# Low parts of weights, of the first columns and the additions of norms: all on VectorE

## The chip, the core and the metric

The kernel runs as one program on one core of a Trainium2 chip. The metric is the device time of one execution in microseconds (us), the median over several runs. On the core five engines work side by side, each with its own queue of instructions: TensorE (PE in the profile; PEld is its weight load), VectorE (DVE), ScalarE (ACT), GpSimd (POOL) and SyncE (SP), which here only issues DMAs. An engine takes its queue in order and waits on semaphores for what other engines produce.

## The reference

A decoder trunk of two layers over 512 tokens of width 1024, in float32. Each layer is: a norm modulated by a condition `c`, a token mixer, a gated residual; then a modulated norm, a mixture of experts (16 experts, two for each token, SwiGLU of width 256), a gated residual. Layer 0 mixes by dilated attention in three head groups (48 heads of 64, one projection of 1024 to 9216 columns), layer 1 by forgetting attention (16 heads, projection to 3088 columns).

```python
for i in range(DEPTH):
    mod = (ada_in @ w_ada[i] + b_ada[i]).reshape(b, 6, d)
    ...
    hm = rmsnorm(x, norm_mix[i]) * (1 + sc_m) + sh_m
    y = dilated_mixer(hm, ...) if i % 2 == 0 else forgetting_mixer(hm, ...)
    x = x + g_m * y
    hf = rmsnorm(x, norm_ffn[i]) * (1 + sc_f) + sh_f
    x = x + g_f * hierarchical_moe(hf, ...)
```

## The kernel before, in words

Every large matrix product is made of three: an operand is split into a high part `hi`, the value rounded to a shorter format by an ACT copy, and a low part `lo` = value - `hi`, and PE adds hi by hi, lo by hi and hi by lo in one PSUM bank (`part`, lines 291 to 298; the line says which of the three a matmul is: 295, 296, 298). So each weight piece of 128 x 1024 that comes from memory needs one ACT instruction (line 150) and one subtraction (line 153) before PE can use it.

`Stream` (line 78) brings the weight pieces in a fixed order: `fetch` issues the DMA on SP's queue into one of a few buffers (`raw`, four of them, in the mixers; more kinds in the experts' stages), `split` makes `hi` and `lo` in six buffers each. A piece is split as soon as fewer than six split pieces are live, that is when PE has let go of an older one (`done`, which calls `fill`). The buffer `raw` is free for the next DMA when both the copy and the subtraction have read it. In the experts' stages all subtractions are on VectorE; in the mixers every second piece (odd `ns`) goes to GpSimd.

The four `raw` buffers also serve `ada` (line 384), a background job that computes the modulation rows: eight DMAs of `w_ada`, eight VectorE multiply-adds (line 394) into `acc`, then a hi/lo split of `acc` (lines 399 and 400) and four matmuls with a column of ones (lines 406 and 409). Ten such jobs run beside mixer A, one instruction group at every second step of the main work.

`begin` (line 301) is the start: x is transposed to columns `xT`, while VectorE adds up 32 half pieces of `w_ada` (line 361) for the first two modulation rows. When a half of them is in, `col` is made (lines 373 and 375), and for four of the eight column blocks ACT makes `hi` (line 378), VectorE the modulated value (line 379), and VectorE or GpSimd `lo` (line 380; GpSimd for blocks 0, 1, 3, 4, 6 and 7).

`normed` (line 420) is a norm over rows: square and sum on ACT, an inverse root in five small instructions (`rsqrt`, lines 215 to 219, two on ACT and three on VectorE, where line 217 multiplies a small tile by itself), a multiply on VectorE (428 or 431) and the addition of the shift row (432). `moe_norm` uses it for four row blocks ahead of each experts' stage, with the addition on GpSimd; the result goes to memory, from where each expert's rows are gathered. `mix_in` uses it for four row blocks of layer 1, with the addition on GpSimd for blocks 1 and 3; PE transposes the result (line 450). In the attention parts `qknorm` (line 458) uses the same `rsqrt` on 128 x 8 tiles.

GpSimd also issues the gathers and scatters of the experts (lines 1198 and 1240), clears `acc` (389), multiplies in the merge of mixer A (789) and does small routing work (1029 to 1182).

The order within each engine's queue is not simply that of the program text. The framework that builds the program simulates it with modelled times and puts, engine by engine, what is ready and first in program order next; where work of several row blocks is independent it ends up interleaved. `issue_after` binds an instruction behind another. So an instruction that moves to another engine may also shift its neighbours in the queues.

Of the kernel before, what the change touches and what calls it, by code (L numbers as in the profile page):

```python
# [8 lines left out]
F32 = mybir.dt.float32  # L9
# [4 lines left out]
OP = mybir.AluOpType  # L14
# [63 lines left out]
class Stream:  # L78
# [51 lines left out]
    def split(self):  # L130
        nc, t = self.t.nc, self.t
        _, n, kind = self.pieces[self.ns]
        tag, raw = self.raws.pop(self.ns)
        if kind == "down":

            self.whole[self.ns] = tag
            self.parts[self.ns] = (raw, None)
            self.ns += 1
            return
        self.held[tag] -= 1  # L140
        self.live += 1
        hi = t.w.tile([P, 1024], F32R, name="hi", tag="hi", bufs=6)
        lo = t.w.tile([P, 1024], F32R, name="lo", tag="lo", bufs=6)
        h, l, r = hi[:, :n], lo[:, :n], raw[:, :n]
        if kind[:3] == "out":

            g = t.g_m[:, int(kind[3:]):int(kind[3:]) + 512].unsqueeze(1).to_broadcast([P, n // 512, 512])
            rv = r.rearrange("p (k c) -> p k c", c=512)
            nc.vector.tensor_tensor(rv, rv, g, op=OP.mult)
        t.act = nc.scalar.activation(h, r, AF.Copy)  # L150
        on_v = kind == "moe" or self.ns % 2 == 0
        eng = nc.vector if on_v else nc.gpsimd
        eng.tensor_tensor(l, r, h.bitcast(F32), op=OP.subtract)  # L153
        self.parts[self.ns] = (hi, lo)
        self.ns += 1

# [21 lines left out]
class Trunk:  # L178
# [122 lines left out]
    def begin(self, sb, first):  # L301

        nc, i, V = self.nc, self.i, self.nc.vector
# [5 lines left out]
        xs = []  # L309
        for b in range(NB):  # L310
            x = self.k.tile([P, D], F32, name="big", tag="big", bufs=5)
# [20 lines left out]
        xT = sb.tile([P, KT, S], F32, name="xT")  # L332

        def rows():
            ss = self.small(NB, "ss4")
            for b in range(NB):
                sq = sb.tile([P, D], F32, name="sq0", tag="sq0", bufs=1)
                nc.scalar.activation(sq, xs[b], AF.Square, accum_out=ss[:, b:b + 1])
            V.tensor_scalar(ss, ss, 1.0 / D, EPS, op0=OP.mult, op1=OP.add)
            r = self.rsqrt(ss, NB)  # L340
            for b in range(NB):
                nc.scalar.activation(xs[b], xs[b], AF.Copy, scale=r[:, b:b + 1])
            for k in range(KT):
                t = self.bank("t")
                for b in range(NB):
                    nc.tensor.transpose(t[:, b * P:(b + 1) * P], xs[b][:, k * P:(k + 1) * P], self.ident)
                nc.scalar.activation(xT[:, k, :], t, AF.Copy)

        wv = i["w_ada"][0].rearrange("(k p) c -> p k c", p=P)
        for half in range(2):  # L350
            cs = slice(half * 512, half * 512 + 512)
            for n in range(2):
                for kk in range(0, KT, 2):
                    if (8 * half + 4 * n + kk // 2) % 11 < 6:
                        raw = self.k.tile([P, D], F32, name="mix", tag="mix", bufs=6)
                    else:
                        raw = sb.tile([P, D], F32, name="ada", tag="ada0", bufs=5)
                    raw = raw.rearrange("p (k c) -> p k c", c=512)
                    nc.sync.dma_start(out=raw, in_=wv[:, kk:kk + 2, (1 - n) * D + half * 512:(1 - n) * D + half * 512 + 512])
                    for k in range(2):  # L360
                        last = V.scalar_tensor_tensor(accs[n][:, cs], raw[:, k], self.csil[:, kk + k:kk + k + 1], accs[n][:, cs], op0=OP.mult, op1=OP.add)
                if half == 0 and n == 0:
                    rows()
            if half:
                self.early = self.project_early(first)
            c = slice(4 * half, 4 * half + 4)
            for n in range(2):
                t = self.bank("s")
                for k in range(4 * half, 4 * half + 4):
                    nc.tensor.matmul(t[:, k:k + 1], lhsT=accs[n][:, k * P:(k + 1) * P], rhs=self.ones[:, 0:1], start=True, stop=True)  # L370
                with self.tc.issue_after(last.ins):
                    if n == 0:
                        V.scalar_tensor_tensor(col[:, 0, c], t[:, c], 1.0, col[:, 0, c], op0=OP.add, op1=OP.mult)
                    else:
                        V.tensor_copy(col[:, 1, c], t[:, c])
            for k in range(4 * half, 4 * half + 4):
                hi, lo = self.h(k, slice(None))
                nc.scalar.activation(hi, xT[:, k, :], AF.Identity, scale=col[:, 0, k:k + 1], bias=col[:, 1, k:k + 1])
                V.tensor_scalar(xT[:, k, :], xT[:, k, :], col[:, 0, k:k + 1], col[:, 1, k:k + 1], op0=OP.mult, op1=OP.add)
                (V if k % 3 == 2 else nc.gpsimd).tensor_tensor(lo, xT[:, k, :], hi.bitcast(F32), op=OP.subtract)  # L380
            if half == 0:
                self.st.fill(2)

# [663 lines left out]
    def moe_norm(self, layer, sb, xs, b, after):  # L1047

        nc, m = self.nc, self.m
        nc.sync.dma_start(out=self.x_d[layer][b * P:(b + 1) * P, :], in_=xs[b])  # L1050
        hf = sb.tile([P, D], F32, name="hf", tag=("xh", "xl")[b], bufs=2) if b < 2 else m["xr"][b - 2]
        m["r", b] = self.normed(xs[b], m["a_f"], m["sh_f"], hf, hf, eng=nc.gpsimd, after=after)
        nc.sync.dma_start(out=self.hf_d[b * P:(b + 1) * P, :], in_=hf)

    def moe_turn(self, sb, xs, b, h):
# [273 lines left out]

    def mix_in(self, layer, b, sb, x, a, sh):  # L1330
        h = sb.tile([P, D], F32, name="hm", tag=("xh", "xl")[b % 2], bufs=2)
        self.normed(x, a, sh, h, h, eng=(self.nc.vector, self.nc.gpsimd)[b % 2])
        c = slice(b * P, (b + 1) * P)
        self.turned(h, 2, lambda k, tv: self.hilo(*(t[:, :, c] for t in self.hT[k // 2]), tv))

# [69 lines left out]
```

## Time and profile before

| what | us |
|---|---|
| median of 3 runs | 1470.24 (1465.14 to 1475.07) |
| the profiled execution | 1476.0 |
| its span on the core | 1474.2 |
| PE busy | 1328.8 (90%) |
| VectorE busy | 966.6 (66%) |
| ScalarE busy | 652.1 (44%) |
| GpSimd busy | 294.9 (20%) |

The span is the time from the first to the last instruction in the profile. Busy time is the union of the instructions' spans on an engine. Matmuls overlap each other, so a busy PE is not a PE at its peak, but where it is idle nothing is being multiplied. The stages in the span: the start to about 65 us, mixer A to 700, its experts to 940, the change to layer 1 to 985, mixer B to 1258, its experts to the end.

### The profile page before, as it was taken

The numbers are of one execution on the slowest core, as the hardware profiler recorded it, in microseconds if no ns is written. First come the engines' busy times: TensorE is split into PE (matmuls) and PEld (weight loads), VectorE is DVE, ScalarE is ACT, GpSimd is POOL, SyncE is SP. The second block draws the span as 40 slices with busy tenths as digits, with TensorE's granted clock in tenths as the row PEclk, the third lists the DMA queues.
The fourth block names the chain that finished last, engine by engine and source line by source line (L and its number), as shares of the span: only waits on it lengthen the run. The fifth ranks groups of instructions, "written<-read, shape, count | busy, mean of one in ns | idle before, by whom it ended". The sixth has DMA issues, their size and how long they took to land. (4 is left out here: it accounts for less than half of the span.)

```text
span 1474.2 us, 20070 instructions
## 1 busy us (share of the span) xinstructions
PE 1328.8 (90%) x7017; PEld 1075.1 (73%) x7017; DVE 966.6 (66%) x1841; ACT 652.1 (44%) x1356; POOL 294.9 (20%) x192
## 2 busy tenths in 40 slices
PE   5799999989998999999969998499999999799995
PEld 3688888868986988887756665268888878566663
DVE  6775766675666675664677775376766753877772
ACT  6333544344433453344245554344544542355551
POOL 2312111221121211110232221211111100332221
PEclk9899999999999999999979999799999999889998
DMA  9356444644454645254679998604222463799981
GB/s 358 117 174 203 143 138 139 192 124 153 145 156 158 188 131 176 68 187 132 232 257 302 283 294 253 179 17 123 72 66 86 133 197 125 253 293 311 306 279 24
DMA packets 187156, 264.15 MB, mean 179 GB/s; under 512 B 23064, under 2 KB 148696, under 8 KB 187046
## 3 DMA queue, kind: packets, MB, share of 16 engines
q1 hardware_dynamic: 160742, 227.86, 47.5%
q0 software_dynamic: 8576, 16.85, 4.9%
q10 hardware_dynamic: 17728, 18.05, 4.1%
q8 instruction: 59, 0.97, 0.3%
q14 instruction: 51, 0.42, 0.1%
HBM read 249.85 MB, written 25.43 MB: 187 GB/s over the span
## 5 line engine op out<-in xcount | busy, mean ns | idle before, releaser
L295 PE MATMUL ps_pj<-hi,h 128*128 128x512 f32 (+1 forms) x1016 | 395.5, 398 | 6.2 <-ACT h L455 3.3
L296 PE MATMUL ps_pj<-lo,h 128*128 128x512 f32 (+1 forms) x1016 | 375.6, 378 | 0.8 <-POOL lo L153 0.8
L298 PE MATMUL ps_pj<-hi,h 128*128 128x512 f32 (+1 forms) x1016 | 290.0, 375 | 5.5 <-POOL h L380 5.4
L153 POOL TENSOR_TENSOR lo<-raw,hi 128x1024 fp32r<-128x1024 f32 x56 | 139.9, 2498 | 620.3 <-ACT hi L150 567.2
L295 PEld LDWEIGHTS ps_pj<-hi,h 128*128 128x128 f32 x1016 | 239.7, 236 | 31.5 <-issue 6.6
L296 PEld LDWEIGHTS ps_pj<-lo,h 128*128 128x128 f32 x1016 | 241.1, 237 | 16.6 <-POOL lo L153 1.4
L298 PEld LDWEIGHTS ps_pj<-hi,h 128*128 128x128 f32 x1016 | 212.1, 236 | 27.3 <-POOL h L380 7.8
L394 DVE SCALAR_TENSOR_TENSOR acc<-ada,csil,acc 128x1024 f32<-128x1024 f32 x80 | 111.9, 1399 | 112.5 <-DMA ada<-in_w_ada 112.2
L150 ACT ACTIVATE hi<-raw 128x1024 fp32r<-128x1024 f32 x126 | 132.2, 1051 | 100.0 <-PE ps_pj L298 52.1
L153 DVE TENSOR_TENSOR lo<-raw,hi 128x1024 fp32r<-128x1024 f32 x70 | 102.8, 1471 | 33.0 <-ACT hi L150 30.0
L295 PE MATMUL ps_pj<-hi,xh 128*112 128x512 f32 x256 | 105.4, 412 | 0.0
L296 PE MATMUL ps_pj<-lo,xh 128*112 128x512 f32 x256 | 104.0, 406 | 0.0
L298 PE MATMUL ps_pj<-hi,xl 128*112 128x512 f32 x256 | 80.9, 397 | 0.0
L1237 DVE SCALAR_TENSOR_TENSOR y<-ps_s,r_ws,g_f 112x512 f32<-112x512 f32 x64 | 47.9, 748 | 35.0 <-PE ps_s L1236 35.0
L455 ACT ACTIVATE xh<-ps_t 128x448 fp32r<-128x448 f32 x64 | 31.8, 542 | 84.3 <-PE ps_t L450 84.3
L462 ACT ACTIVATE sq<-ps_pj 128x512 f32<-128x512 f32 x63 | 37.0, 589 | 61.8 <-PE ps_pj L298 50.9
L927 DVE CUSTOM_DVE_ANT_0 nl<-ps_s,cums 128x128 f32<-128x128 f32 (+1 forms) x64 | 31.0, 484 | 46.5 <-PE ps_s L925 43.4
L153 DVE TENSOR_TENSOR lo<-h,hi 128x1024 fp32r<-128x1024 f32 x42 | 51.1, 1223 | 15.6 <-ACT hi L150 14.7
L722 PEld LDWEIGHTS ps_o<-vr,pt 128*128 128x128 f32 x480 | 58.0, 192 | 1.4
L929 ACT ACTIVATE nl<-nl,mn 128x128 f32<-128x128 f32 (+1 forms) x64 | 35.8, 559 | 50.6 <-DVE mn L927 50.0
L722 PE MATMUL ps_o<-vr,pt 128*128 128x64 f32 x480 | 57.3, 271 | 0.0
L464 DVE TENSOR_REDUCE qss<-sq 128x8 f32<-128x512 f32 x64 | 43.4, 679 | 20.0 <-ACT sq L462 19.7
(283 smaller groups left out, 2306.7 us busy)
## 6 DMA issues: line engine op xcount, KB each, us to landing
ada<-in_w_ada SPq DMA_DIRECT2D x85, 512.0 KB
raw<-in_a_w_in SPq DMA_DIRECT2D x128, 256.0 KB
h<-in_w_gate SPq DMA_DIRECT2D x42, 256.0 KB
h<-in_w_up SPq DMA_DIRECT2D x42, 256.0 KB
mix<-in_w_gate SPq DMA_DIRECT2D x37, 256.0 KB
mix<-in_w_up SPq DMA_DIRECT2D x37, 256.0 KB
raw<-in_w_down SPq DMA_DIRECT2D x18, 512.0 KB
h<-in_w_down SPq DMA_DIRECT2D x18, 512.0 KB
```

Of the source, the lines that this page charges most:

```text
L150: t.act = nc.scalar.activation(h, r, AF.Copy)
L153: eng.tensor_tensor(l, r, h.bitcast(F32), op=OP.subtract)
L295: nc.tensor.matmul(out, lhsT=hi, rhs=wh, start=first and n == 0, stop=False)
L296: nc.tensor.matmul(out, lhsT=hi, rhs=wl, start=False, stop=False)
L298: nc.tensor.matmul(out, lhsT=lo, rhs=wh, start=False, stop=last and n == len(terms) - 1)
L394: nc.vector.scalar_tensor_tensor(acc, raw, self.csil[:, kt:kt + 1], acc, op0=OP.mult, op1=OP.add)
L455: self.nc.scalar.activation(hv, tv, AF.Copy)
L462: nc.scalar.activation(sq, ps, AF.Square)
L464: nc.vector.tensor_reduce(ss, sq.rearrange("p (h d) -> p h d", d=HD), axis=AX.X, op=OP.add)
L722: nc.tensor.matmul(held["o"][:, at:at + HD], lhsT=pt[:, a * P:(a + 1) * P], rhs=v, start=(m == 0), stop=(m == len(terms) - 1))
L929: nc.scalar.activation(pr[:, sl], pr[:, sl], AF.Exp, scale=-1.0, bias=mn, accum_out=held["d"][:, h * 4 + b:h * 4 + b + 1])
L1237: nc.vector.scalar_tensor_tensor(y[:, cs], yp, m["ws"][0:CAP, e:e + 1], m["g_f"][0:CAP, cs], op0=OP.mult, op1=OP.mult)
```

## The change

Four lines choose VectorE where the kernel before chose GpSimd in some cases. Nothing else is edited.

```diff
@@ split
-        on_v = kind == "moe" or self.ns % 2 == 0
-        eng = nc.vector if on_v else nc.gpsimd
-        eng.tensor_tensor(l, r, h.bitcast(F32), op=OP.subtract)
+        nc.vector.tensor_tensor(l, r, h.bitcast(F32), op=OP.subtract)
@@ begin
-                (V if k % 3 == 2 else nc.gpsimd).tensor_tensor(lo, xT[:, k, :], hi.bitcast(F32), op=OP.subtract)
+                V.tensor_tensor(lo, xT[:, k, :], hi.bitcast(F32), op=OP.subtract)
@@ moe_norm
-        m["r", b] = self.normed(xs[b], m["a_f"], m["sh_f"], hf, hf, eng=nc.gpsimd, after=after)
+        m["r", b] = self.normed(xs[b], m["a_f"], m["sh_f"], hf, hf, after=after)
@@ mix_in
-        self.normed(x, a, sh, h, h, eng=(self.nc.vector, self.nc.gpsimd)[b % 2])
+        self.normed(x, a, sh, h, h)
```

## Rows read from the trace of the kernel before

**Rows 1.** Page, busy time of each engine: us, share of the span, instructions.
```profile
PE 1328.8 (90%) x7017; PEld 1075.1 (73%) x7017; DVE 966.6 (66%) x1841; ACT 652.1 (44%) x1356; POOL 294.9 (20%) x192
```

**Rows 2.** Windows: us, busy time by engine, granted clock, DMA share, GB/s.
```profile
46.00:54.00 8.00, 4.79 (x14) 3.58 (x14) 5.05 (x7) 5.50 (x7) 3.66 (x2) 0.57 0.21 69
200.00:400.00 200.00, 186.50 (x1019) 166.74 (x1020) 134.33 (x271) 86.61 (x221) 35.66 (x20) 0.97 0.48 148
```

**Rows 3.** Waits of PE: line, what ended it, us in total, times, longest.
```profile
PE ps_s L406 <- ACT ada L399: 20.3, 9, 3.7
...
PE ps_s L1120 <- DVE r_act L1114: 6.4, 2, 3.2
PE ps_t L657 <- DVE qn L470: 5.8, 5, 2.4
PE ps_pj L298 <- POOL h L380: 5.4, 4, 2.0
...
PE ps_s L370 <- DVE col L373: 2.9, 1, 2.9
...
PE ps_t L450 <- POOL hm L432: 1.4, 1, 1.4
```

**Rows 4.** Lines of POOL by form: count, busy us, mean ns, idle before.
```profile
L153 POOL TENSOR_TENSOR lo<-raw,hi 128x1024 fp32r<-128x1024 f32 x56 | 139.9, 2498 | 620.3 <-ACT hi L150 567.2 <-DMA ada<-in_w_ada 53.1
...
L380 POOL TENSOR_TENSOR h<-xT,h 128x512 fp32r<-128x512 f32 x6 | 10.0, 1680 | 26.0 <-DVE xT L379 26.0
L432 POOL TENSOR_TENSOR hf<-hf,sh_f 128x1024 f32<-128x1024 f32 x4 | 9.5, 2387 | 64.8 <-DVE ss L425 59.1 <-DVE hf L431 5.7
```

**Rows 5.** Lines of DVE by form, same columns.
```profile
L394 DVE SCALAR_TENSOR_TENSOR acc<-ada,csil,acc 128x1024 f32<-128x1024 f32 x80 | 111.9, 1399 | 112.5 <-DMA ada<-in_w_ada 112.2
L153 DVE TENSOR_TENSOR lo<-raw,hi 128x1024 fp32r<-128x1024 f32 x69 | 102.5, 1488 | 33.0 <-ACT hi L150 30.0 <-DMA fall_d<-r_fall 2.4
L153 DVE TENSOR_TENSOR lo<-h,hi 128x1024 fp32r<-128x1024 f32 x42 | 51.1, 1223 | 15.6 <-ACT hi L150 14.7
...
L217 DVE TENSOR_TENSOR rs_t<-rs_y 128x8 f32<-128x8 f32 x64 | 30.2, 472 | 18.4 <-ACT rs_y L216 17.8
...
L219 DVE SCALAR_TENSOR_TENSOR rs_y<-rs_t,rs_y 128x8 f32<-128x8 f32 x64 | 10.3, 162 | 1.5
...
L431 DVE SCALAR_TENSOR_TENSOR hf<-big,rs_y,a_f 128x1024 f32<-128x1024 f32 x4 | 5.1, 1280 | 0.1
...
L1109 DVE TENSOR_TENSOR r_og<-r_og,r_mx 128x8 f32<-128x8 f32 x4 | 4.7, 1186 | 0.0
...
L432 DVE TENSOR_TENSOR hm<-hm,row 128x1024 f32<-128x1024 f32 x2 | 2.4, 1220 | 0.0
```

**Rows 6.** Timeline at 99 to 105 us: start, us, instruction, idle before.
```profile
99.22 2.86 POOL L153 TENSOR_TENSOR lo<-raw,hi 128x1024 fp32r<-128x1024 f32 x1 [22.84 <-ACT hi L150]
...
99.73 2.37 DVE L217 TENSOR_TENSOR rs_t<-rs_y 128x8 f32<-128x8 f32 x1
...
104.66 0.30 PE L657 MATMUL ps_t<-J,qn 128*128 128x128 f32 x1 [2.36 <-DVE qn L470]
```

**Rows 7.** Timeline of DVE in the start.
```profile
27.64 3.46 DVE L361 SCALAR_TENSOR_TENSOR acc<-ada,csil,acc 128x512 f32<-128x512 f32 x2
31.03 3.04 DVE L379 TENSOR_SCALAR xT<-xT,col 128x512 f32<-128x512 f32 x2
33.98 0.68 DVE L380 TENSOR_TENSOR h<-xT,h 128x512 fp32r<-128x512 f32 x1
...
38.75 7.46 DVE L361 SCALAR_TENSOR_TENSOR acc<-mix,csil,acc 128x512 f32<-128x512 f32 x10
...
57.93 0.99 DVE L379 TENSOR_SCALAR xT<-xT,col 128x512 f32<-128x512 f32 x2
```

**Rows 8.** Waits of DVE: line, what ended it, us in total, times, longest.
```profile
DVE acc L394 <- DMA ada<-in_w_ada: 112.2, 54, 5.5
DVE lo L153 <- ACT hi L150: 74.4, 74, 5.0
```

## The prediction

> **What bounds the kernel now.** I read the page's busy times first: PE works 90% of the span, VectorE 66%, POOL 20% [rows 1]. In mixer A VectorE is busy 134 of 200 us and PE 186 [rows 2]. So the kernel is bound by PE, and a change to VectorE and POOL can move only the 145 us in which PE is idle. The waits of PE come next [rows 3]: look at who ends them. POOL does so in two places that count, the columns of the start (5.4 us) and one norm at the change of layer (1.4). The larger waits lie behind ScalarE and VectorE: 20.3 us at the end of the background jobs, 6.4 in the two routings, 5.8 in the query and key norms. Then the groups by line, for what the moved instructions cost on either engine [rows 4, 5], and there one thing stands out that decides the case: the same VectorE subtraction has a mean of 1488 ns on `raw` in the mixers, where POOL works too, and 1223 ns on `h` among the experts, where POOL subtracts nothing. Line 217, which handles eight numbers per partition, has a mean of 472 ns where its neighbour, line 219, has 162. The timeline shows why [rows 6]: a line 217 that starts 0.5 us into a POOL subtraction takes 2.37 us and ends when POOL ends, and 5 us later PE has stood still for 2.36 us behind that norm. VectorE is held while POOL subtracts.
>
> **The change part by part.** *Work moved.* 56 subtractions of weights at 1.223 us are 68.5 us; 6 of columns at 0.68 [rows 7] are 4.1; 10 additions (four such rows of norms, then four and two more) at 1.22 are 12.2. VectorE gets 85 us. POOL loses 139.9 + 10.0 and 10 times about 2.39, some 174 us [rows 4], and no DMA moves.
>
> *Time given back.* From group means against an undisturbed row of like shape [rows 5]: line 153 on `raw` (1488 - 1223) x 69 = 18.3 us; line 394 (1399 - 1280, as line 431) x 80 = 9.5; line 217 (472 - 162) x 64 = 19.8; line 1109 (1186 - 162) x 4 = 4.1. In the start two pairs: line 361 3.46 against a fifth of 7.46, so 2.0; line 379 3.04 against 0.99, so 2.0 [rows 7]. Together 56 us, a lower bound, since small groups are left out. VectorE's busy time grows by at most 85 - 56 = 29 us, 3% of 967. POOL is then no engine for anything in the mixers but the clearing of `acc` and the merge.
>
> Now what lies on PE's path, by stage.
>
> *Second half of the start.* PE waits 5.4 us for line 380 on POOL, four times [rows 3], 1.68 us an instruction against 0.68 on VectorE: four times 1.0 shorter is 4.0. But VectorE then has three more weight subtractions between them. Bounds: 5.4 gained, 2 lost (three times 1.22, less a 1.68 no longer waited for). I take 3.0, nearer to the four times 1.0.
>
> *First half of the start.* VectorE runs without a break towards line 373, for which PE waits 2.9 us. Added: three columns and one weight piece, 3 x 0.68 + 1.22 = 3.3; given back 4.0. So 0.7 gained, between 2.9 and -3.3.
>
> *Change of layer.* One addition that PE waits 1.4 us for becomes 1.22 instead of some 2.39: 1.1 gained, between 1.4 and -1.2 (it delays the next block's root).
>
> *The two routings.* In each, one line 1109 stands behind POOL's last addition for some 2.05 us (4.1 over two), and PE waits 3.2 behind that chain. The addition itself, 1.22, now stands in that queue. If it goes ahead: 0.8 each, 1.7 gained. If the planner puts it behind the routing: 4.1. If the hold went on without POOL: -2.4. I take 1.7. The gather reads these rows from memory, but waits for the routing's indices later than for them.
>
> *Mixers.* About 52 of the 56 subtractions lie here: 64 us added, 47.6 given back, so VectorE's load is nearly as it was, in pieces of 1.2 us instead of holds of up to 2.2. Gain at most the 5.8 us of the query norms and the 9.5 that line 394 is held, 15.3. Loss at most the 16 us of net work plus the waits in the next paragraph. I take the one case shown [rows 6], 2.4, and a sixth of the 9.5 (most of line 394's lateness is its DMA, 112 us [rows 8]): 4.0.
>
> *What is queued behind.* A subtraction on VectorE waits for its `hi` on ScalarE: 74.4 us over the 184 full-size ones [rows 8], 0.40 each, so 56 more would wait 22 us, with the logits and norms behind them in the queue. I count nothing for it, because VectorE is idle a third of these stages [rows 2]; with that cover gone it costs all 22. [...]
>
> *Buffers and queues.* A `raw` buffer is let go 1.2 us earlier for the odd pieces, so SP issues the next DMA earlier; I cost this at nothing, since DMA is half idle there (0.48).
>
> Sum: 3.0 + 0.7 + 1.1 + 1.7 + 4.0 = 10.5 us. The profiled execution took 1476.0, 5.8 above the median: 1465.5 in its terms, **1460** beside the median of 1470.2.
>
> **The rivals.** *More comes back* (all upper bounds): 5.4 + 0.7 + 1.4 + 4.1 + 15.3 = 27 us, 1443. For it: the hold hits small instructions in chains that PE waits for. [...] Against it: the 20.3 us behind the background jobs are mostly DMA.
> [...]
>
> *Nothing stays.* The 6.5 us outside the mixers come, and the mixers lose as much, because the order in all queues is planned anew around 72 moved instructions and the net work on VectorE is a little more: 1470.
>
> *Slower, VectorE's queue becomes the late one.* In the mixers 16 us net and 52 x 0.40 = 21 us of waiting for `hi` make VectorE 37 us later; if two thirds of that (its busy share there) reach PE, 25 are lost against 6.5 gained, so 1470 + 18 = 1488. It decides where the moved subtractions stand ahead of logits and norms whose bank PE needs next. For it: one queue for everything, waits of up to 5.0 us [rows 8]. Against it: half of the pieces go this way already, and line 153 ends almost none of PE's waits.
>
> That the change doesn't do what it says is no rival: the four lines name the engine outright.
>
> **How the numbers follow.** Forecast 0.42, more 0.24, nothing 0.20, slower 0.14. Within 1% of 1470.2 is 1455.5 to 1484.9, about what a measurement can tell from no change. The forecast's own range is 1450 to 1470; some 0.16 of its 0.42 lies under 1455.5, and all of the first rival. Faster 0.24 + 0.16 = 0.40; same 0.26 + 0.20 = 0.46; slower 0.14. The range 1440 to 1484 leaves out most of the slower case and a few hundredths under 1440.
>
> **What would show it.** Line 153 on `raw` at about 1.23 us in one group of 125 or so, line 217 near 0.17, line 1109 near 0.16; VectorE's busy time 975 to 1000 us, POOL's about 120; no wait of PE ended by POOL's lines 380, 432 or 153; line 1120's wait about 2.4 each. The forecast is wrong if waits of PE ended by VectorE's lines 470, 927, 691 or 662 grow by over 10 us, if VectorE's wait for `hi` grows well past 22 us, or if line 406's 20 us change by more than 5 either way.

## The result, and the profile after

The changed kernel takes 1432.89 us (median of 4 runs, 1427.06 to 1437.23) against 1470.88 before: ratio 0.9731, 95% interval 0.9703 to 0.9759, so 38 us or 2.7% faster. The forecast was 1460, the range 1440 to 1484. The direction was right, the size was not: the gain is between three and four times the 10.5 us of the sum, and outside the range.

The page of the changed kernel, busy us by engine:

```profile
PE 1311.6 (92%) x7017; PEld 1068.2 (75%) x7017; DVE 967.4 (68%) x1913; ACT 652.4 (46%) x1356; POOL 121.0 (8%) x120
```

The span and the mean granted clock, from its view of the cores (1474.2 us and 0.952 before):

```profile
core 0: 1425.3 us, clock 0.966
```

Beside [rows 1]: POOL lost 174 us, as worked out. VectorE took 72 more instructions, 85 us of work, and is busy for the same 967 us as before, so about as much was given back. PE is idle for 114 us instead of 145, and its 7017 matmuls take 17 us less, at a higher granted clock (0.966 against 0.952). These two make the 49 us by which the profiled execution is shorter (1474.2 to 1425.3; it is the fastest of the four, and the others had a clock of 0.958 to 0.964, so the medians differ by 38 us only).

Lines of VectorE by form in the changed kernel: count, busy us, mean ns, idle before. The changed file is two lines shorter above most of these, so 394 is now 392, 217 is 215, 1109 is 1107.

```profile
L151 DVE TENSOR_TENSOR lo<-raw,hi 128x1024 fp32r<-128x1024 f32 x125 | 151.5, 1221 | 45.1 <-ACT hi L150 43.2 <-DMA ada<-in_w_ada 1.0
L392 DVE SCALAR_TENSOR_TENSOR acc<-ada,csil,acc 128x1024 f32<-128x1024 f32 x80 | 102.6, 1283 | 69.0 <-DMA ada<-in_w_ada 68.8
...
L215 DVE TENSOR_TENSOR rs_t<-rs_y 128x8 f32<-128x8 f32 x64 | 10.4, 164 | 22.1 <-ACT rs_y L214 21.2
...
L1107 DVE TENSOR_TENSOR r_og<-r_og,r_mx 128x8 f32<-128x8 f32 x4 | 0.6, 158 | 0.0
```

Every hold of [rows 5] is gone: 1488 to 1221 ns, 472 to 164, 1186 to 158. Compared instruction by instruction with the median of its form, VectorE lost some 76 us in the trace before (62 of them while POOL subtracted weights) and 3 in the one after; the prediction's 56 was a lower bound, and said so.

Waits of PE in the changed kernel, to be read beside [rows 3].

```profile
PE ps_s L404 <- ACT ada L397: 10.8, 6, 3.1
PE ps_s L1118 <- DVE r_act L1112: 5.5, 2, 2.8
```

No wait ended by POOL's arithmetic is left. The largest change is one that the forecast held fixed: the waits at the end of the background jobs fall from 20.3 to 10.8 us.

Now the view that the prediction did not read, the waits of SP's queue, which issues the weight DMAs. First the kernel before, then the changed one; a row says which issue waited, for whom, us in total, times, longest.

```profile
SPq L114 <- POOL lo L153: 211.8, 35, 29.9
...
SPq L114 <- DVE lo L153: 124.9, 63, 14.2
...
SPq L393 <- POOL lo L153: 30.1, 13, 4.9
...
SPq L393 <- DVE lo L153: 17.8, 8, 5.3
```

```profile
SPq L114 <- DVE lo L151: 199.5, 85, 16.4
...
SPq L391 <- DVE lo L151: 30.7, 21, 11.1
```

An issue needs a free `raw` buffer, and that is free when the copy and the subtraction have read it. Before, SP stood 337 us for weight pieces (211.8 + 124.9) and 48 for pieces of the background jobs behind subtractions; after, 200 and 31. While it stood for the longest of these, 29.9 us for one POOL subtraction (from 1072.0 to 1101.9 us in the trace before), it issued nothing. Such a wait is not a loss by itself, because pieces are fetched ahead. But VectorE's wait for the DMAs of the jobs fell with it, from 112 us to 69 in line 392's row.

Where the time came from, by landmarks that both programs have (start of the instruction in each trace, us from the span's start):

| PE reaches | before | after | gained so far |
|---|---|---|---|
| first transpose of a query (end of the start) | 72.9 | 64.1 | 8.8 |
| fourth background job | 257.6 | 244.0 | 13.6 |
| tenth background job | 576.1 | 546.7 | 29.4 |
| first routing | 747.2 | 713.9 | 33.3 |
| first norm of layer 1 | 955.6 | 917.0 | 38.6 |
| second routing | 1281.3 | 1231.8 | 49.5 |
| end | 1474.2 | 1425.3 | 48.9 |

The gain grows through both mixers, some 24 us between the start and the first routing and 11 in mixer B. Single traces differ by several us where nothing differs (below, 10 us between two that time the same), so only the large steps are read.

### The profile page after: what moved, and what is told of

Its sections match the earlier page's. It is cut to its first block, busy times and chain, and to the rows that moved or that the text cites. A ratio compares the mean times of both kernels' runs of the same rounds, so it can differ in the third digit from the quotient of the medians.

```text
span 1425.3 us, 20009 instructions
## 1 busy us (share of the span) xinstructions
PE 1311.6 (92%) x7017; PEld 1068.2 (75%) x7017; DVE 967.4 (68%) x1913; ACT 652.4 (46%) x1356; POOL 121.0 (8%) x120
## 3 DMA queue, kind: packets, MB, share of 16 engines
q1 hardware_dynamic: 160742, 227.86, 48.9%
## 5 line engine op out<-in xcount | busy, mean ns | idle before, releaser
L151 DVE TENSOR_TENSOR lo<-raw,hi 128x1024 fp32r<-128x1024 f32 x126 | 151.8, 1213 | 48.1 <-ACT hi L150 46.1
L392 DVE SCALAR_TENSOR_TENSOR acc<-ada,csil,acc 128x1024 f32<-128x1024 f32 x80 | 102.6, 1283 | 69.0 <-DMA ada<-in_w_ada 68.8
L293 PEld LDWEIGHTS ps_pj<-hi,xh 128*112 128x112 f32 x256 | 45.5, 178 | 15.4 <-ACT xh L453 3.1
L296 PEld LDWEIGHTS ps_pj<-hi,xl 128*112 128x112 f32 x256 | 44.9, 176 | 15.6 <-DVE xl L454 0.6
```

The costliest lines, as they stand in the source:

```text
L151: nc.vector.tensor_tensor(l, r, h.bitcast(F32), op=OP.subtract)
L293: nc.tensor.matmul(out, lhsT=hi, rhs=wh, start=first and n == 0, stop=False)
L296: nc.tensor.matmul(out, lhsT=lo, rhs=wh, start=False, stop=last and n == len(terms) - 1)
L392: nc.vector.scalar_tensor_tensor(acc, raw, self.csil[:, kt:kt + 1], acc, op0=OP.mult, op1=OP.add)
```

## The experiments

Theory H: what the change gave back is the time in which VectorE is held while POOL subtracts. Theory L: the other half of it is lateness, since a subtraction on POOL takes 2.4 us, behind others in POOL's queue, and so the low part and the `raw` buffer are let go late. Theory P: neither counts for much, and it is the order of all queues, planned anew, that came out better. Unless a note says otherwise an edit is to the changed kernel, and ratios are to the kernel before, so 0.9731 is no change and 0.0100 of a ratio is 14.7 us. By their intervals the difference of two ratios is uncertain by 6 to 8 us, and each difference below has to be read with that. The expectations use 0.44 and 0.16 us for a held and a worked us, from differences of medians; the ratios, taken each beside its own runs of the kernel before, give the 0.55 and 0.2 of the text.

### The parts alone

`e2_rest_only`: the columns and the additions on VectorE, the weights' subtractions chosen as in the kernel before.

```diff
-        nc.vector.tensor_tensor(l, r, h.bitcast(F32), op=OP.subtract)
+        on_v = kind == "moe" or self.ns % 2 == 0
+        eng = nc.vector if on_v else nc.gpsimd
+        eng.tensor_tensor(l, r, h.bitcast(F32), op=OP.subtract)
```

> Columns and additions of norms on VectorE, the 56 subtractions of weights still on GpSimd. Theory H (what the change gave back is the time in which VectorE is held by GpSimd's subtractions of weights): most holds stay, so only the start, the change of layer and the routings gain, 6 to 12 us, ratio to before 0.992 to 0.997, and VectorE's line 217 (128x8) keeps its mean near 0.47 us. Theory L (what cost was the late low part: 2.4 us on GpSimd instead of 1.2, buffers let go late): the same. Theory P (the gain is the new order of all queues, whatever moved): any ratio, as likely as not below 0.98.

Measured: 1468.79 us, ratio 0.9971 (0.9942 to 1.0000), about 4 us. VectorE's lines by form in it, same columns as above:

```profile
L394 DVE SCALAR_TENSOR_TENSOR acc<-ada,csil,acc 128x1024 f32<-128x1024 f32 x80 | 112.5, 1407 | 105.9 <-DMA ada<-in_w_ada 105.1 <-issue 0.6
...
L217 DVE TENSOR_TENSOR rs_t<-rs_y 128x8 f32<-128x8 f32 x64 | 30.3, 473 | 18.2 <-ACT rs_y L216 17.7
```

The holds stay as they were. `e1_stream_only` is the other part: the kernel before with only the first of the four edits.

> Only the 56 subtractions of weights on VectorE, columns and norms as before. All theories: 1470 - 34 = 1436 to 1439, ratio 0.975 to 0.979, if the two parts add up; P would allow a miss of 1%.

Measured: 1438.51 us, ratio 0.9777 (0.9734 to 0.9821). The parts add up (4 and 33 us), and the 56 subtractions are most of the gain.

### Is it the order of the queues?

`e3_parity`, an edit to the kernel before:

```diff
-        on_v = kind == "moe" or self.ns % 2 == 0
+        on_v = kind == "moe" or self.ns % 2 == 1
```

> The kernel before with the roles of even and odd pieces swapped: as many subtractions on GpSimd, each in another place, and with that another order of the queues. Theories H and L: the same load and as many holds, ratio 0.995 to 1.005. Theory P: an order that differs is worth about what the change gave beyond the holds, so 1% or more either way.

Measured: 1471.91 us, ratio 0.9998 (0.9966 to 1.0031), although queues differ in hundreds of places. Its trace has a span of 1464.0 against 1474.2, the 10 us of scatter meant above. This replanning cost nothing, against theory P; the next two runs settle more, because their queues are the changed kernel's but for five instructions of VectorE in the second.

### Holds alone

`e4_pool_reads`: POOL reads and nobody waits for it.

```diff
         nc.vector.tensor_tensor(l, r, h.bitcast(F32), op=OP.subtract)
+        if kind != "moe" and self.ns % 2 == 1:
+            d = t.w.tile([P, 320], BF16, name="dum", tag="dum", bufs=1)
+            for c in (0, 320, 640):
+                nc.gpsimd.tensor_tensor(d, h.bitcast(F32)[:, c:c + 320], h.bitcast(F32)[:, c:c + 320], op=OP.subtract)
```

> The changed kernel, and beside each odd weight piece of the mixers GpSimd makes three useless subtractions of 320 columns that read the high part (about 2.5 us together); nobody waits for their result. All useful work stays on VectorE. Theory H: VectorE is held as before the change and also carries the work, so at least all of the gain is lost: ratio to before 0.995 to 1.03, line 217 again at 0.4 us or more. Theory L: low parts and buffers come as early as in the changed kernel, ratio 0.970 to 0.982. Theory P: unknown, but the holds themselves cost nothing much: under 0.985.

Measured: 1451.47 us, ratio 0.9887 (0.9862 to 0.9912), 0.0156 or some 23 us above the changed kernel. PE, VectorE, ScalarE and SP run exactly the instructions of the changed kernel in exactly its order. From its lines by form:

```profile
L155 POOL TENSOR_TENSOR dum<-hi 128x320 bf16<-128x320 f32 x168 | 198.9, 1184 | 623.2 <-ACT hi L150 591.9 <-ACT rs_y L218 22.3
...
L151 DVE TENSOR_TENSOR lo<-raw,hi 128x1024 fp32r<-128x1024 f32 x125 | 163.3, 1315 | 35.2 <-ACT hi L150 33.7
L396 DVE SCALAR_TENSOR_TENSOR acc<-ada,csil,acc 128x1024 f32<-128x1024 f32 x80 | 105.3, 1316 | 68.7 <-DMA ada<-in_w_ada 67.8 <-DMA acc<-in_b_ada 0.5 <-issue 0.2
...
L219 DVE TENSOR_TENSOR rs_t<-rs_y 128x8 f32<-128x8 f32 x64 | 14.8, 232 | 18.4 <-ACT rs_y L218 17.5
```

Which lines of VectorE are held shows in two groups. The first two rows are one group in the kernel before and in the changed one, the last two another:

```profile
L470 DVE TENSOR_TENSOR qn<-ps_pj,rs_y 128x512 f32<-128x512 f32 x63 | 43.2, 686 | 1.5
L468 DVE TENSOR_TENSOR qn<-ps_pj,rs_y 128x512 f32<-128x512 f32 x63 | 43.1, 686 | 1.1
...
L379 DVE TENSOR_SCALAR xT<-xT,col 128x512 f32<-128x512 f32 x8 | 7.6, 976 | 1.0 <-ACT h L378 1.0
L377 DVE TENSOR_SCALAR xT<-xT,col 128x512 f32<-128x512 f32 x8 | 4.1, 542 | 0.0
```

A line that reads its large input from PSUM (`ps_pj`) keeps its 686 ns (684 in `e4_pool_reads`). The line that scales and shifts one tile of SBUF is held, 976 ns before against 542 after (690 in `e4_pool_reads`), so lines with two large inputs are not the only ones.

Holds are shown to cost PE's time. No wait of PE or ScalarE in this trace is ended by POOL's useless subtractions, so it is not the high part's buffer that they keep. The holds are shorter here, 42 us in all by the count against the median of each form, since each useless subtraction is only 1.2 us long. The background jobs' DMAs come as early as in the changed kernel (67.8 us of waiting). A held subtraction also lets its `raw` buffer go later: SP stands 222 us for weights and 44 for the jobs' pieces behind subtractions, against 200 and 31 in the changed kernel, so a part of the 23 us may come that way. All three theories missed: H said that at least all of the gain goes.

`e5_pool_writes`: POOL busy at the same places, but writing.

```diff
         nc.vector.tensor_tensor(l, r, h.bitcast(F32), op=OP.subtract)
+        if kind != "moe" and self.ns % 2 == 1:
+            d = t.w.tile([P, 320], BF16, name="dum", tag="dum", bufs=1)
+            nc.gpsimd.tensor_copy(d[:, 0:4], h.bitcast(F32)[:, 0:4])
+            for _ in range(8):
+                nc.gpsimd.memset(d, 0.0)
```

> As the kernel with useless subtractions, but beside each odd piece GpSimd copies four columns of the high part and then clears 320 columns eight times, so that it is busy for about as long at the same places and reads almost nothing. Theory H, if only GpSimd's reading holds VectorE: ratio to before 0.970 to 0.980 as the changed kernel, line 217 at 0.17 us. If writing holds it too: 0.995 to 1.03. Theory L: 0.970 to 0.980. Together with the kernel that reads, this tells a busy GpSimd from a GpSimd that reads.

Measured: 1434.77 us, ratio 0.9759 (0.9733 to 0.9785), not told apart from the changed kernel.

```profile
L156 POOL MEMSET dum<- 128x320 bf16 x448 | 164.8, 368 | 25.9
L154 POOL CAST dum<-hi 128x4 bf16<-128x4 f32 x56 | 51.8, 925 | 589.2 <-ACT hi L150 565.3 <-ACT rs_y L219 23.5
...
L220 DVE TENSOR_TENSOR rs_t<-rs_y 128x8 f32<-128x8 f32 x64 | 10.5, 165 | 21.6 <-ACT rs_y L219 20.8
```

POOL is busy for 217 us in these lines, more than its 140 before the change, and VectorE's small multiply keeps its 165 ns. So in these two runs it is not a busy POOL that holds VectorE, but one that subtracts and so reads (the same multiply took 232 ns in `e4_pool_reads`); a POOL instruction with a single large input was not tried.

### VectorE's time as such

`e6_v_twice`:

```diff
         nc.vector.tensor_tensor(l, r, h.bitcast(F32), op=OP.subtract)
+        if kind != "moe" and self.ns % 2 == 1:
+            nc.vector.tensor_tensor(l, r, h.bitcast(F32), op=OP.subtract)
```

> The changed kernel with each odd subtraction of the mixers made twice on VectorE: 56 x 1.22 = 68 us more of planned work there, about what the holds took before, and no hold. Theory H in the form 'VectorE's time is what counts, hold or work': the gain is lost, ratio to before 0.99 to 1.01. Theory H in the form 'holds hurt because they strike unplanned, the small steps of chains': VectorE's spare third takes most of it, ratio 0.975 to 0.988. Theory L: low parts come 1.2 us later on every odd piece, half of the change's effect on them: 0.98 to 0.99.

Measured: 1443.72 us, ratio 0.9819 (0.9794 to 0.9844), 0.0088 or 13 us for 68 us of work. The extra instructions by form:

```profile
L153 DVE TENSOR_TENSOR lo<-raw,hi 128x1024 fp32r<-128x1024 f32 x56 | 68.2, 1219 | 0.2
```

A microsecond of VectorE's planned work costs about 0.2 us here, one of holding about 0.55 (23 by 42). This says why the change gains although VectorE is as busy as before. The 0.2 is not the price of work alone, though. The second subtraction reads the `raw` piece again, so that low part and buffer are let go later too, as the expectation under theory L said, and SP stands 285 us for weights behind subtractions (200 in the changed kernel):

```profile
SPq L114 <- DVE lo L151: 146.6, 61, 16.6
SPq L114 <- DVE lo L153: 138.6, 35, 29.7
```

So the 13 us hold both, and no run here separates them. The queues' order also differs from the changed kernel's in this run.

### Lateness

`e9_late`: low part and buffer let go about as late as on POOL, with hardly a hold. What is useful stays on VectorE; POOL makes four columns once more.

```diff
         nc.vector.tensor_tensor(l, r, h.bitcast(F32), op=OP.subtract)
+        if kind != "moe" and self.ns % 2 == 1:
+            d = t.w.tile([P, 320], BF16, name="dum", tag="dum", bufs=1)
+            nc.gpsimd.tensor_copy(d[:, 0:4], h.bitcast(F32)[:, 0:4])
+            for _ in range(3):
+                nc.gpsimd.memset(d, 0.0)
+            nc.gpsimd.tensor_tensor(l[:, 0:4], r[:, 0:4], h.bitcast(F32)[:, 0:4], op=OP.subtract)
```

> The changed kernel, but of each odd weight piece of the mixers GpSimd makes the low part of the first four columns once more, behind a small copy and three clearings, so that the low part and the buffer are let go about 2.4 us after the high part, as when GpSimd subtracted, and VectorE is hardly held. So far: the 56 subtractions are worth 34 us (the kernel with the rest alone gained 4), and GpSimd's reading brought back 18.6 of them with all queues in the same order. Theory L (the rest, some 15 us, is the lateness of low part and buffer): ratio to before 0.982 to 0.988. Theory H (holds alone): 0.972 to 0.978. Theory P (the rest is the order of the queues): 0.972 to 0.978.

Measured: 1453.78 us, ratio 0.9879 (0.9836 to 0.9922), 0.0148 or 22 us above the changed kernel. The order of the queues is the changed kernel's but for some two dozen of PE's 7017 instructions and a few others; the holds come to 3 us, as in the changed kernel. Waits of SP's queue, then of VectorE:

```profile
SPq L114 <- POOL lo L157: 200.7, 34, 29.4
...
SPq L114 <- DVE lo L151: 106.7, 57, 11.9
...
SPq L397 <- POOL lo L157: 28.3, 17, 4.5
```

```profile
DVE acc L398 <- DMA ada<-in_w_ada: 89.4, 52, 4.1
```

SP stands 307 us for weights behind subtractions again. Theory L holds, and lateness alone costs as much here as the holds did in `e4_pool_reads`. Two runs split it. `e11_raw_late` replaces the last line by one that reads the buffer and leaves the low part alone, `e12_lo_late` by one that rewrites the low part and leaves the buffer alone:

```diff
-            nc.gpsimd.tensor_tensor(l[:, 0:4], r[:, 0:4], h.bitcast(F32)[:, 0:4], op=OP.subtract)
+            nc.gpsimd.tensor_copy(d[:, 0:4], r[:, 0:4])                                                    # e11
+            nc.gpsimd.tensor_tensor(l[:, 0:4], l.bitcast(F32)[:, 0:4], t.ones[:, 0:4], op=OP.mult)         # e12
```

> As the kernel with late parts (ratio 0.988, 20 us over the changed kernel), but only the buffer is late: GpSimd's last small instruction reads four columns of the raw piece and writes a scratch tile, so the low part is ready as in the changed kernel. If the buffer is what counts (the next DMAs, of weights and of the background jobs, are issued later): ratio to before 0.984 to 0.991, and VectorE's line of the background jobs waits some 90 us for its DMA, as there, against 69 in the changed kernel. If the low part is what counts: 0.972 to 0.978 and 69.

> The other half: GpSimd's last small instruction multiplies four columns of the low part by one, in place, and does not touch the raw piece. PE gets the low part late, the buffer is free early. If the low part counts: ratio 0.984 to 0.991. If the buffer counts: 0.972 to 0.978, and the wait of the background jobs' line for its DMA near 69 us.

Measured: 1447.75 us, ratio 0.9847 (0.9803 to 0.9890) with the buffer late, and 1437.58, 0.9774 (0.9742 to 0.9806), with the low part late. So the buffer is the larger part, some 17 us of the 22, and the low part 6, which its interval cannot tell from nothing. Beside each other, with the same number of instructions on POOL, the two runs differ by 10 us. The order of `e12_lo_late` is as near to the changed kernel's as that of `e9_late`; in `e11_raw_late` some 60 of PE's and 40 of VectorE's instructions stand elsewhere. SP's waits in `e11_raw_late`, then in `e12_lo_late`:

```profile
SPq L114 <- DVE lo L151: 265.9, 85, 28.3
...
SPq L114 <- POOL dum L157: 37.7, 25, 2.6
```

```profile
SPq L114 <- DVE lo L151: 198.4, 86, 17.2
```

304 us against 198, where the changed kernel has 200. The expectation that the jobs' DMA wait would tell them apart was wrong: it is 88.1 us in the one and 81.4 in the other.

`e10_pool_again`: everything at once, the whole odd subtraction a second time on POOL.

```diff
         nc.vector.tensor_tensor(l, r, h.bitcast(F32), op=OP.subtract)
+        if kind != "moe" and self.ns % 2 == 1:
+            nc.gpsimd.tensor_tensor(l, r, h.bitcast(F32), op=OP.subtract)
```

> The changed kernel, and each odd subtraction of the mixers is made a second time on GpSimd over all 1024 columns, into the same low part: full holds, the full lateness and GpSimd's queue as before the change, with VectorE's work as after it. Theory H: the holds of 65 us in place of the 42 of the kernel with useless reading give 1433 + 0.44 x 65 = 1462, ratio 0.990 to 0.997. Theory H with L: another 10 to 15, so 1472 to 1478, ratio 1.000 to 1.006. Theory P: what does not come back of 34 us plus the price of VectorE's extra work (11 us by the kernel that subtracts twice there) is the order: 0.985 to 0.990.

Measured: 1486.62 us, ratio 1.0087 (1.0060 to 1.0114), 0.0356 or 52 us above the changed kernel and 13 above the one before. Holds of 71 us by the same count, at 0.55, are 39 us; with the 22 of lateness that is 61, more than the 52, but within what the intervals of these prices allow. The ratio lies just above the range of theory H with L (1.000 to 1.006), and far from those of the other two. What POOL's subtraction costs is more than the whole gain; VectorE's own 68 us of work, at most 13 us by `e6_v_twice`, are the price paid for being rid of it.

### A better version?

`e8_more_v` moves the rest of the elementwise work in the mixers to VectorE: the merge's multiplication, the router's two products and the small products of `rank`, each by writing `nc.vector` for `nc.gpsimd`:

```diff
-            nc.gpsimd.tensor_tensor(o0, o0, w4(e0), op=OP.mult)
+            nc.vector.tensor_tensor(o0, o0, w4(e0), op=OP.mult)
...
```

> The changed kernel with what is left on GpSimd of elementwise work in the mixers on VectorE too: the multiplication in the merge (4 x 1.9 us there, which holds VectorE's own multiplication beside it from 1.2 to 2.9 us) and the small routing products. Theory H: 7 us of holds go, 5 us of work come, at 0.44 and 0.16 us each: 2 us faster than the changed kernel at best, ratio to before 0.970 to 0.976. A new order of the queues may hide it.

Measured: 1432.46 us, ratio 0.9731 (0.9704 to 0.9758). `e13_copies` adds to it:

```diff
-        if self.nev % 2:
+        if self.nev % 4:
             self.nc.scalar.activation(out, in_, AF.Copy)
```

> As the kernel with more on VectorE, and of the copies out of PSUM in the attention parts, which alternate between ScalarE and VectorE, three of four go to ScalarE, some 17 us off VectorE. At 0.16 us for each us of planned work there, 3 us faster, less what ScalarE loses (46% busy): ratio to before 0.966 to 0.976. If it is faster than the changed kernel by over 0.5%, it is the better version.

Measured: 1430.74 us, ratio 0.9731 (0.9701 to 0.9761). Neither is told apart from the changed kernel, which stays the version to use.

## Why the prediction was wrong

**The step that failed** is the one under "Buffers and queues": "I cost this at nothing, since DMA is half idle there". The `raw` buffer is let go earlier, as it said, and the DMA share did not show what that is worth: it is 0.48 before the change and 0.49 in the same stage after it (186.4 to 372 us). What stood was SP, 337 us in all behind subtractions on weights' buffers and up to 29.9 us for a single one, in which it issued nothing. Letting the buffer go late again cost 17 us (`e11_raw_late`, 9 to 25 by its interval and the changed kernel's; 10 beside `e12_lo_late`), and SP's waits show that its issues stood behind it (304 us against 200). The waits of SP's queue were not read before the sum was made; 211.8 us there stood behind the very instructions that the change moves.

**The term that was mis-sized** is "Mixers", 4.0 us within bounds of 15.3 gained and 37 lost. The weights' part measured about 33 us (0.9777), nearly all of it there. The mechanism, holds, was right and is shown by `e4_pool_reads`. But the term counted a hold only where PE's idle time stood in a row right behind it, one of 2.4 us, and a sixth of line 394's; by the 0.55 us for each us held, the 62 us before the change cost an estimated 34. And the upper bound left lateness out, so it was no bound. Set against that are at most 13 us of VectorE's own work. 34 + 22 - 13 = 43 is more than the measured 33; the intervals of the three prices together allow that, but as the 13 hold some lateness too, the sum with work alone would be higher still. Each part is shown to cost PE time by itself; how the 33 us divide between them is not shown.

**PE's idle time alone was too narrow a bound** for what the change can move. Of the 49 us between the traces 31 are idle time and 17 are matmuls that run in less time; the granted clock rose from 0.952 to 0.966, and busy time times clock stayed the same (1265 and 1267). The prediction's sum has no term for the clock.

**Start, change of layer, routings**: 6.5 us forecast, 4 measured (`e2_rest_only`, 0 to 9 by its interval). PE's wait for the routing fell by 0.4 each, not 0.8; the addition does stand ahead of line 1112, for which PE waits, as taken.

**What is queued behind**: the wait of the subtractions for `hi` rose from 74.4 [rows 8] to 84.0 us, 10 and not 22, and VectorE's spare time covers most of its additional work, at most 13 us of 68 reaching PE. So the choice to count nothing was nearly right. With the 22 us counted in full the sum would have come out slower than before. VectorE's order in `e4_pool_reads` is that of the changed kernel although its instructions were held (line 219 at 232 ns against 164), so nothing overtook there; but what stood in the queue cost less than the holds that it replaced.

**The rivals**: the first, "more comes back", is the nearest, 1443, and was still 10 us short. Its sum calls all its terms upper bounds but takes 0.7 for the first half of the start, where the bound was 2.9; with that it comes to 29 us and 1441. "Nothing stays" did not come, and `e3_parity` shows one replanning at no cost. "Slower" made VectorE 37 us later in the mixers; its busy time did not grow, and its waits for `hi` grew by 10 us.

**What would show it**: every row came as said but three. The wait at line 1120 is 2.75 us each and not 2.4. VectorE's busy time is 967 and not 975 or more, because the 56 us given back were a lower bound; and line 406's wait, which the forecast needed to stay within 5 us, fell by 9.5. That earlier buffers did this is not shown.

**What stays open**: through which DMAs a late buffer reaches PE. Weights and background jobs share the four buffers. PE's waits at the end of the jobs are 10.8 us in the changed kernel and 16.9 with the buffer late (`e11_raw_late`), 6 us of the 17; but they are 14.7 with the buffer early and the low part late (`e12_lo_late`), so they do not account for it. And a late buffer need not cost that much: `e6_v_twice` has nearly as much waiting of SP for weights (285 us against 304), but only 4.0 us of PE's waits at the end of the jobs, and the lateness together with 68 us of work cost 13. Buffers of the jobs' own were not tried.

## What to carry to other kernels

A subtraction on GpSimd was not free here just because GpSimd was idle for 80% of the span. It held VectorE's instructions that read their inputs from SBUF (1488 ns against 1221 for the weights' subtractions), down to those of eight numbers in chains that PE waits for (472 against 164), and a held microsecond cost an estimated 0.55 us, a worked one 0.2. Look in VectorE's lines for a mean far above that of a neighbour of like shape. And when an instruction moves, read who waits for its inputs to be released, in the waits of the queue that issues the DMAs, before putting its speed at nothing.

## What was not expected of the hardware

An instruction of 8 columns that reads one and the same tile twice was held too: 472 ns in the mean before, 164 after. GpSimd was slower in turn where VectorE worked beside it: of its useless subtractions of 320 columns in `e4_pool_reads`, the 33 that overlapped no VectorE instruction with two inputs from SBUF took 737 ns in the mean, the other 135 took 1293. And a GpSimd that only wrote, 448 clearings of 368 ns, cost nothing that the runs can tell.
